# All of ff2 through the seven products, with weight sums added by DMA

## The chip, the cores and the metric

The kernel runs on 1 core of a Trainium2 chip. The metric is the device time of one execution in microseconds; below it is that of the profiled execution and the median of three others. TensorE (PE) multiplies, VectorE (DVE) and ScalarE (ACT) work element by element, GpSimd (POOL) does a few small operations, and transfers are issued by SyncE (SP) and carried by 16 DMA engines.

## The reference, cut to what matters

One layer on 512 tokens of 1024 channels: a gated pair of attention branches, a squared-ReLU MLP with 4096 hidden channels, a gated per-layer embedding, and norms between them. All is float32.

```python
u = rms_norm(h, g_mix[i])
z = u @ w_in[i]                      # q, k, v of both branches, forget logits, 2 x 1024 gate logits
# y_a, y_b: the two attention branches, each projected to 1024
gates = jax.nn.sigmoid(gate_logits).reshape(B, S, N_BRANCH, D_MODEL)
mixed = gates[:, :, 0] * y_a + gates[:, :, 1] * y_b
h = h + mixed @ w_mix_out[i]
u = rms_norm(h, g_mlp[i])
h = h + jnp.square(jax.nn.relu(u @ w_ff1[i])) @ w_ff2[i]      # 1024 -> 4096 -> 1024
ple_gate = jax.nn.sigmoid(rms_norm(h, g_ple[i]) @ w_ple_gate[i])
h = h + ple_gate * (p[i] @ w_ple_proj[i])
return rms_norm(h, g_final)
```

## The kernel before, in words

Every operand of a matmul is split into a high and a low half (`hi_lo`, lines 72 to 75: ScalarE casts the high half, VectorE subtracts for the low one), and a product is three passes: high times high, high times low, low times high (`mm3`). A weight is loaded by SP into a raw tile (`emit_dma`, lines 221 to 237), and `emit_split` (278 to 303) makes its two halves in `w_hi` and `w_lo`, tiles with four buffers each. A *unit* is one such weight; `order` is their sequence, `advance(i)` splits up to unit i, and `look["n"]` counts the units split. Raw tiles are 1 MB and stand in two rings of two (`w_raw`, `w2_raw`); loads are asked for three units ahead.

Some large products go through a scheme with seven products in place of eight: input and weight are cut into 2 x 2 blocks, seven sums of blocks are multiplied (numbers 1 to 7, `pn`), and three accumulators x, y and z in PSUM collect them (`win_mm`, `win_out`). The sums of weight blocks are made by VectorE in `sum_source` (251 to 276), one 1024-column operation each: two for product 6, one each for 7 and 4. The gates' upper half (`P2_STEPS`) and all of ff1 work so.

The MLP is done in four quarters `fq` of 1024 hidden channels, each two groups of 512 (`2 * fq` and `2 * fq + 1`). ff1 of both groups takes 14 products of 24 matmuls with 256 columns. `ff1_act` applies ReLU and square on ScalarE, `ff1_lo` makes the low halves and, for the even group, the sums that ff2's seven products need. ff2 of the even group takes seven products (`s2_mm`, 12 matmuls of 512 columns each); ff2 of the odd group is done plainly (`ff2_mm`): 4 row blocks by 2 halves, 12 matmuls each, in the same or a fourth accumulator. `h_add` adds the accumulators to `h_sb` on VectorE. In the last quarter the plain part goes by row blocks, so that the squares for the last norm (`part_ssq`) and the transposes `t3` follow block by block; then come the gate products `psgt` with the weights `wpg`.

The order on PE and POOL is written out by hand; `FIRST_STEPS` and `NEXT_STEPS` (lines 45 to 50) give that of the products, and in the loop of lines 1283 to 1322 step n splits the units up to step n + 2 and forms sums up to n + 3. ACT, DVE and SP are ordered by a planner, except in the stretches under `manual_schedule` (lines 1264 to 1322 up to n = 2, among others). Ahead of the loop stands the entry: the last row block of the mix product, the transposes of the normed rows (`t2_pe`), the sums of their blocks (`t2_sums`, `t2_sums2`, `t2_rest`, partly on POOL) and the embedding product (`pp_half`), whose results `ppo` are spilled and reloaded as `pp`.

Of the kernel before, what the change touches and what calls it, by code (L numbers as in the profile page):

```python
# [14 lines left out]
P = 128  # L15
# [29 lines left out]
FIRST_STEPS = ((1, 1), (0, 1), (0, 2), (1, 2), (0, 6), (0, 5), (0, 7), (1, 6), (0, 4), (0, 3),  # L45
               (1, 7), (1, 5), (1, 4), (2, 1), (1, 3), (2, 6), (2, 2), (2, 5), (2, 7), (2, 3),
               (2, 4))
NEXT_STEPS = ((0, 1), (0, 2), (0, 6), (1, 1), (1, 2), (0, 7), (0, 5), (0, 4), (0, 3), (1, 6),
              (2, 1), (1, 7), (1, 5), (2, 2), (1, 4), (1, 3), (2, 6), (2, 5), (2, 7), (2, 3),
              (2, 4))  # L50
# [4 lines left out]
def layer_kernel(ctx: ExitStack, tc: tile.TileContext, x, p, g_mix, w_in, b_forget, swa_sinks,  # L55
# [52 lines left out]
    def ff_steps(fq):  # L108


        a, b = 2 * fq, 2 * fq + 1
        first = [("s2", fq, pn) if i == 2 else ("f1", (a, b)[i], pn)
                 for i, pn in (NEXT_STEPS if fq else FIRST_STEPS)]
        last = []
        if fq < 3:
            last += [("f2", fq, ((half, j),), range(NT)) for half in range(2) for j in range(2)]
        else:
            last += [("f2", fq, ((0, 0), (0, 1), (1, 0), (1, 1)), (tb,)) for tb in range(NT)]
        return first + last

    steps = [st_ for fq in range(4) for st_ in ff_steps(fq)]
# [22 lines left out]
    def blocks(w, r0, c0, name):  # L144

        return [add_raw([(slice(0, 4), w[r:r + 512, c0:c0 + 512]
                          .rearrange("(k q) c -> q k c", q=P))], [P, 4, 512], f"{name}_{r}")
                for r in (r0, r0 + 512)]
# [23 lines left out]
    for fq in range(4):  # L172
        gw = {}
        for g in (2 * fq, 2 * fq + 1):
            gw[g] = blocks(w_ff1, 0, g * 512, f"wf1_{g}")
        c2 = [add_raw([(slice(0, 4), w_ff2[fq * 1024:fq * 1024 + 512, ch * 512:ch * 512 + 512]
                        .rearrange("(k q) c -> q k c", q=P))], [P, 4, 512], f"wf2_{fq}_{ch}")
              for ch in range(2)]
        f2 = [rows(w_ff2, fq * 1024 + 512, ch * 512, f"wf2b_{fq}_{ch}") for ch in range(2)]
        for st_ in ff_steps(fq):  # L180
            if st_[0] == "f1":
                add(st_, (gw[st_[1]], st_[2], [P, 4, 2, P]))
            elif st_[0] == "s2":
                add(st_, (c2, st_[2], [P, 2, 512]))
            else:
                for half, j in st_[2]:
                    if ("f2", fq, half, j) not in unit_of:
                        add(("f2", fq, half, j), f2[half][j])
# [5 lines left out]
    look = {"t2": None, "split": 2, "dma": 4, "wp2": None, "n": 0, "d": 0}  # L194

    def raws_of(i):
        r, pn = order[i][1][:2]
        if not isinstance(r, list):
            return [r]
        if order[i][0][0] in ("f1", "g"):  # L200
            return {1: r[:1], 2: r[1:], 3: r[1:], 4: r[1:]}.get(pn, r)
        return {1: r[:1], 2: r[:1], 3: r[1:], 4: r[:1], 5: r[:1], 7: r[1:]}.get(pn, r)
# [12 lines left out]
    in_wp2, same = [], {True: [], False: []}  # L215
    for n, r in enumerate(used):
        in_wp2.append(n >= first_raw[first_block] and (n - first_raw[first_block]) % 4 > 1)
        same[in_wp2[n]].append(n)
    before = {n: s_[z - 2] for s_ in same.values() for z, n in enumerate(s_) if z >= 2}

    def emit_dma(i):

        upto = max(first_raw[r] for r in raws_of(i))
        while look["d"] <= upto:
            n = look["d"]
            if n in before and last_use[used[before[n]]] >= look["n"]:
                return
            r = raws[used[n]]
            if in_wp2[n]:
                if look["wp2"] is None:  # L230
                    return
                r["tile"] = look["wp2"].tile(r["shape"], F32, tag="w2_raw", bufs=2, name=r["name"])
            else:
                r["tile"] = wp.tile(r["shape"], F32, tag="w_raw", bufs=2, name=r["name"])
            for ks, src in r["fns"]:
                nc.sync.dma_start(r["tile"][:, ks, :], src)
            look["d"] += 1

    def quadrant(i, h, e):

        rs = order[i][1][0]
        if order[i][0][0] in ("f1", "g"):
            t = raws[rs[h]]["tile"].rearrange("q k (j e c) -> q k j e c", e=2, c=P)
            return t[:, :, :, e]
        return raws[rs[e]]["tile"][:, h:4:2, :]
# [3 lines left out]
    def sum_source(i):  # L251

        if i in sources or i >= len(order) or not isinstance(order[i][1][0], list):
            return
        emit_dma(i)
        rs, pn, _ = order[i][1]

        first = {6: 1, 4: 2}.get(pn)
        if (first and unit_of[order[i][0][:-1] + (first,)] >= look["n"]
                or pn in (4, 7) and unit_of[order[i][0][:-1] + (6,)] not in sources  # L260
                or any(raws[r]["tile"] is None for r in raws_of(i))):
            return
        if pn == 6:
            b11, b12, b22 = quadrant(i, 0, 0), quadrant(i, 0, 1), quadrant(i, 1, 1)
            t1 = sources[unit_of[order[i][0][:-1] + (5,)]] = look.pop("t1", b11)
            nc.vector.tensor_tensor(t1, b12, b11, ALU.subtract)
            sources[i] = raws[rs[0]]["t2"] = look["t2"](order[i][1][2], f"t2_{i}")
            nc.vector.tensor_tensor(sources[i], b22, t1, ALU.subtract)  # L268
        elif pn == 7:
            b12 = sources[i] = quadrant(i, 0, 1)  # L270
            nc.vector.tensor_tensor(b12, quadrant(i, 1, 1), b12, ALU.subtract)
        elif pn == 4:
            b21 = sources[i] = quadrant(i, 1, 0)
            nc.vector.tensor_tensor(b21, b21, raws[rs[0]]["t2"], ALU.subtract)  # L274
        else:
            sources[i] = quadrant(i, pn in (2, 3), pn == 3)

    def emit_split(i):
# [8 lines left out]
        src = sources[i] if isinstance(r, list) else raws[r]["tile"][sl]  # L287
# [17 lines left out]
    def advance(i):  # L305

        while look["n"] < min(len(order), i + 1):
            emit_split(look["n"])
            look["n"] += 1
            emit_dma(min(len(order) - 1, look["n"] + 3))  # L310
# [32 lines left out]
    def to_uT(xn, uh, ul, tb, trp, name):  # L343

        for half in range(2):
            tr = trp.tile([P, 4, P], F32, tag="tr", bufs=3, name=f"{name}_tr{half}")
# [469 lines left out]

    at2 = ctx.enter_context(tc.tile_pool(name="at2", bufs=1))
# [40 lines left out]
    def win_out(key, pn, new):  # L858
# [30 lines left out]
    look["t2"] = lambda shape, name: hp.tile(shape, F32, tag="gb", bufs=1, name=name)  # L889
# [10 lines left out]
    def gate_ops(z):  # L900
# [21 lines left out]
        nc.vector.tensor_tensor(a12, a12, a22, ALU.subtract)  # L922
# [4 lines left out]
    def gate_out(res, gi):  # L927
# [3 lines left out]
        for j in range(2):  # L931
            m = 4 + 2 * j + e
# [4 lines left out]
            nc.scalar.activation(sgw[gi, m][:, 256 * i:256 * i + 256], src[:, j], AF.Sigmoid)  # L937
# [50 lines left out]
    look["t2"] = lambda shape, name: wk3.tile(shape, F32, tag="t2", bufs=1, name=name)  # L988
# [12 lines left out]
    def h_add(tb, half, ps):  # L1001
        sl = h_sb[:, tb, half * 512:half * 512 + 512]
        nc.vector.tensor_tensor(sl, ps, sl, ALU.add)  # L1003
# [20 lines left out]
    def new_op(pn):  # L1024
        n = (5, 7, 3).index(pn)
        u_op[pn] = [spare(n + 4 * i, f"u2_{pn}{'hl'[i]}", (P, 4, 256)) for i in range(2)]
# [25 lines left out]
    def put(pn, tb, src):  # L1052
        sl = t2_cols(tb)
        hi_lo(u_op[pn][0][sl], u_op[pn][1][sl], src)
# [9 lines left out]
    def t2_sums(tb):  # L1064
# [4 lines left out]
        nc.vector.tensor_tensor(s1, trs[tb, 1], a21, ALU.add)  # L1069
# [3 lines left out]
    def t2_sums2(tb):  # L1073
        a21, s1, s2, s3, s4 = sums[tb]
        nc.vector.tensor_tensor(s2, s1, a_raw[0][t2_cols(tb)], ALU.subtract)
        put(6, tb, s2)
        nc.gpsimd.tensor_tensor(s4, a_raw[1][t2_cols(tb)], s2, ALU.subtract)
# [26 lines left out]
    def pp_half(half):  # L1104

        wh, wl = unit(("pp", half))
        for tb in range(NT):
# [8 lines left out]
            if half == 1:  # L1116
                nc.sync.dma_start(pp_dram[tb], pp_out[tb])

# [315 lines left out]
```

## Time and profile before

| | |
|---|---|
| median of 3 runs | 746.66 us (745.09 to 746.82) |
| profiled execution | 745.08 us, span 743.4 us |
| PE, DVE, ACT, POOL busy | 98%, 74%, 58%, 5% of the span |
| DMA | 87.36 MB in 54584 packets, mean 118 GB/s |

The span runs from the first to the last instruction of the profiled execution; some 1.7 us of its time lie around it. In the rows further down, "a <-b" names the tile written and the tiles read, L is the line of the kernel, and an idle time stands with what ended it. Times in timelines and chains are microseconds from the start of the span.

### The profile page before, as it was taken

Reading aid. Unit: us, or ns where it says so; the run is one execution under the profiler, and the core shown is the slowest. Engines: PE = TensorE matmul, PEld = TensorE weight load, DVE = VectorE, ACT = ScalarE, POOL = GpSimd, SP = SyncE. Lnnn points to the kernel's source line nnn. Section 1 sums busy time; section 2 is a strip of 40 time slices with the busy share of each in tenths; the row PEclk is TensorE's granted clock in tenths of the full one; section 3 lists DMA queues with packets and bytes.
Section 4 is the critical chain, followed back from the end, with each engine's and each line's share of the span. In section 5 each row is a group of like instructions: output and inputs, shape, how many; then the busy total and the mean of one; then the engine's idle time right before and its main releaser. Section 6 shows DMA issues by size and latency. Waiting matters only on the chain.

```text
span 743.4 us, 11230 instructions
## 1 busy us (share of the span) xinstructions
PE 729.8 (98%) x4282; PEld 643.2 (87%) x4282; DVE 549.4 (74%) x906; ACT 431.1 (58%) x814; POOL 38.1 (5%) x71
## 2 busy tenths in 40 slices
PE   8999999999999999999999999999999999999996
PEld 7988888888889998887989889988999889988885
DVE  5656978876799557355989678985889578973654
ACT  6547888789753543335767317752486227754542
POOL 1011301100000000002100000000000000001001
PEclk9999999999999999999999999999999999999998
DMA  8266546550540382430242703252033603472002
GB/s 268 77 169 145 148 106 160 143 156 0 181 160 1 140 324 71 147 114 1 113 142 86 226 2 114 66 177 99 13 123 122 197 1 114 142 233 108 1 1 114
DMA packets 54584, 87.36 MB, mean 118 GB/s; under 512 B 5121, under 2 KB 22017, under 8 KB 54530
## 3 DMA queue, kind: packets, MB, share of 16 engines
q1 hardware_dynamic: 54530, 86.64, 37.1%
q8 instruction: 34, 0.56, 0.3%
q14 instruction: 20, 0.16, 0.1%
HBM read 72.93 MB, written 4.19 MB: 104 GB/s over the span
## 4 chain that ended last, share of the span: by engine, by line
PE 92%; DVE 4%; ACT 1%; DMA 1%; issue 1%; POOL 0%; SPq 0%; POOLq 0%; DVEq 0%; ACTq 0%
PE pf L78 5%; PE pf L80 5%; PE pf L79 5%; PE h_sc L700 2%; PE h_pv L770 2%; PE h_tr L758 2%; PE psm L78 2%; PE psm L80 2%; PE psm L79 2%; PE psy L80 2%; PE psy L78 2%; PE psy L79 2%; PE psgt L80 2%; PE psgt L78 2%; PE psgt L79 2%; PE va L433 2%
## 5 line engine op out<-in xcount | busy, mean ns | idle before, releaser
L718 ACT ACTIVATE s<-s,h_nm 128x128 f32<-128x128 f32 (+1 forms) x64 | 32.6, 512 | 5.9 <-DVE h_nm L711 5.2
L329 POOL TENSOR_SCALAR n_ms<-acc 128x1 f32<-128x1 f32 x15 | 4.9, 325 | 584.1 <-ACT junk L1011 518.2
L75 DVE TENSOR_TENSOR h_ptl<-h_tr,h_pth 128x512 fp32r<-128x512 f32 (+2 forms) x40 | 22.9, 604 | 3.9 <-ACT h_pth L74 3.6
L1011 ACT ACTIVATE junk<-h_sb 128x512 f32<-128x512 f32 x16 | 10.1, 632 | 21.9 <-DVE h_sb L1003 21.9
L74 ACT CAST u_h<-n_tr 128x512 fp32r<-128x512 f32 x22 | 12.3, 584 | 14.7 <-PE n_tr L349 7.8
L74 ACT CAST h_pth<-h_tr 128x512 fp32r<-128x512 f32 (+2 forms) x40 | 19.5, 523 | 1.8 <-PE h_tr L758 1.4
L75 DVE TENSOR_TENSOR u_l<-n_tr,u_h 128x512 fp32r<-128x512 f32 x22 | 14.7, 686 | 7.2 <-ACT u_h L74 7.1
L758 PE MATMUL h_tr<-ident,s 128*128 128x128 f32 x136 | 19.6, 277 | 0.2 <-ACT s L738 0.2
L1003 DVE TENSOR_TENSOR h_sb<-psm,h_sb 128x512 f32<-128x512 f32 x8 | 5.5, 689 | 16.3 <-PE psm L80 16.3
L1340 DVE TENSOR_TENSOR sgp<-sgp,pp 128x512 f32<-128x512 f32 (+1 forms) x9 | 5.7, 632 | 15.8 <-ACT sgp L1339 15.8
L770 PE MATMUL h_pv<-h_pth,v 128*128 128x256 f32 (+1 forms) x64 | 17.3, 291 | 0.0
L770 PE MATMUL h_pv<-h_ptl,v 128*128 128x256 f32 (+1 forms) x64 | 16.9, 305 | 0.4 <-DVE h_ptl L75 0.3
L758 PEld LDWEIGHTS h_tr<-ident,s 128*128 128x128 f32 x136 | 15.1, 141 | 2.0 <-ACT s L738 0.6
L738 ACT ACTIVATE s<-s,h_rec 128x128 f32<-128x128 f32 (+2 forms) x32 | 14.2, 483 | 2.3 <-DVE h_rec L732 2.3
L780 DVE TENSOR_TENSOR h_ao<-h_pv,h_ao 64x512 f32<-64x512 f32 x16 | 10.9, 681 | 6.1 <-ACT h_ao L779 5.8
L268 DVE TENSOR_TENSOR t<-wf,wf 128x1024 f32<-128x1024 f32 x12 | 14.6, 1218 | 0.1
L274 DVE TENSOR_TENSOR wf<-wf,t 128x1024 f32<-128x1024 f32 x12 | 14.6, 1215 | 0.0
L706 DVE CUSTOM_DVE_ANT_0 s<-h_sc,causal 128x128 f32<-128x128 f32 (+3 forms) x32 | 13.8, 483 | 0.3 <-PE h_sc L700 0.3
L732 DVE RECIPROCAL h_rec<-h_den 128x4 f32<-128x4 f32 x16 | 3.0, 185 | 14.5 <-ACT s L718 14.3
L770 PEld LDWEIGHTS h_pv<-h_ptl,v 128*128 128x128 f32 x64 | 12.1, 188 | 1.7 <-DVE h_ptl L75 0.8
L1339 ACT ACTIVATE sgp<-psgt,rs 128x512 f32<-128x512 f32 x7 | 4.8, 688 | 14.7 <-PE psgt L80 14.7
L706 DVE CUSTOM_DVE_ANT_0 s<-h_sc,bswa 128x256 f32<-128x256 f32 (+1 forms) x32 | 10.6, 383 | 3.1 <-PE h_sc L700 3.1
(1756 smaller groups left out, 2944.3 us busy)
## 6 DMA issues: line engine op xcount, KB each, us to landing
wf<-in_w_ff_dram SPq DMA_DIRECT2D x24, 1024.0 KB, 5.2
wf2b<-in_w_ff_dram SPq DMA_DIRECT2D x8, 1024.0 KB, 4.9
wg<-in_w_in_dram SPq DMA_DIRECT2D x4, 1024.0 KB, 5.7
wgw<-in_w_in_dram SPq DMA_DIRECT2D x4, 1024.0 KB, 5.7
wmix<-in_w_mix_out_dram SPq DMA_DIRECT2D x4, 1024.0 KB, 5.3
wpg<-in_w_ple_gate_dram SPq DMA_DIRECT2D x4, 1024.0 KB, 7.3
wv<-in_w_in_dram SPq DMA_DIRECT2D x4, 520.0 KB, 6.1
x<-in_x_dram SPq DMA_DIRECT2D x8, 256.0 KB, 4.5
```

The lines of the kernel that those rows point to most:

```text
L74: nc.scalar.copy(hi, src)
L75: nc.vector.tensor_tensor(lo, src, hi.bitcast(F32), ALU.subtract)
L78: nc.tensor.matmul(ps, lh, rh, start=start, stop=False)
L79: nc.tensor.matmul(ps, lh, rl, start=False, stop=False)
L80: nc.tensor.matmul(ps, ll, rh, start=False, stop=stop)
L268: nc.vector.tensor_tensor(sources[i], b22, t1, ALU.subtract)
L433: nc.tensor.matmul(ps, u[:, kk_, ts_], w[:, kk_, c0:c1], start=kk_ == 0 and n == 0, stop=kk_ == KT - 1 and n == 2)
L700: nc.tensor.matmul(ps[:, off:off + n], qs[i][z][:, qb * P:(qb + 1) * P], kk[i][z][:, k0:k0 + n], start=z == 0, stop=z == 1)
L706: nc.vector.tensor_tensor_reduce(out=s[:, o:o + n], in0=ps[:, off:off + n], in1=c["bias"](qb), scale=1.0, scalar=NEG, op0=ALU.add, op1=ALU ...
L718: nc.scalar.activation(sl, sl, AF.Exp, bias=nm[:, qb:qb + 1], accum_out=den[:, qb:qb + 1])
L758: nc.tensor.transpose(tr[:, n, :], c["s"][:, o, :], ident)
L770: nc.tensor.matmul(pv[:, q0:q0 + nq, :], V2[kb][:, c["v"], :], t[:, o:o + nq, :], start=n == 0, stop=n == 2 * NT - 1, skip_group_check=True)
```

## The change

- `STEPS` replaces the two step lists: per quarter 28 products, a and b being ff1 of the even and odd group, A and B their ff2. Both groups' ff2 goes through the seven products; the odd group adds into the accumulators that the even group began (`s2_mm`), and `h_add` follows only the odd group (`s2_out`). `ff2_mm` and the fourth accumulator go.
- The scheme's signs are turned so that sums of weights are additions. `sum_source` makes each sum in the place of one of its blocks: by a DMA from POOL that adds (`accum_op`), except products 5 and 7 of ff2, which stay on VectorE. The gates' weight sums become such DMAs too. They are formed as soon as the unit is split whose place they take (in `advance`).
- The ff weights come in 512 KB blocks, into twelve places of that size (eight halves of the old raw tiles and `t2`, `c3`, `c7`, `gb`), each given to the next block by the time that it comes free. Loads are asked for eight units ahead in the MLP.
- The operands of ff2 get fixed places `d0` to `d7` and one of `xn`; their sums are formed by `ff2_op` some steps after product 4 of ff1, for both groups.
- In the entry the splits of the first four units and the sums are spread among the row blocks of `pp_half`. The transposes `t3` move: 0 ahead of the last product, 1 behind it, 2 and 3 behind the first two row groups of `psgt`.

```diff
+STEPS = "a1 b1 a2 a5 b5 b2 a6 b6 a7 a3 b7 b3 A1 a4 b4 B1 A2 A5 B5 B2 A6 B6 A3 A7 B7 B3 A4 B4"
...
+    steps = [("f1" if c in "ab" else "s2", 2 * fq + (c in "bB"), int(pn))
+             for fq in range(4) for c, pn in STEPS.split()]
...
+    for g in range(8):
+        ff_blocks["f1", g] = block(w_ff1, 0, g * 512, 4, 256, f"wf1_{g}")
+        ff_blocks["s2", g] = block(w_ff2, g * 512, 0, 2, 512, f"wf2_{g}")
...
+            pl = min(free_at, key=free_at.get)
+            before[r] = free_at[pl]
+            free_at[pl] = last_use[r]
+            place_of[r] = pl
+        elif r >= last_ff:
+            w2 = sum(x >= last_ff for x in used[:n]) < 2
+            z = sum(x >= last_ff for x in used[:n]) % 2
+            before[r] = max(free_at[w2, z, y] for y in range(2))
...
-        if pn == 6:
-            b11, b12, b22 = quadrant(i, 0, 0), quadrant(i, 0, 1), quadrant(i, 1, 1)
-            t1 = sources[unit_of[order[i][0][:-1] + (5,)]] = look.pop("t1", b11)
-            nc.vector.tensor_tensor(t1, b12, b11, ALU.subtract)
-            sources[i] = raws[rs[0]]["t2"] = look["t2"](order[i][1][2], f"t2_{i}")
-            nc.vector.tensor_tensor(sources[i], b22, t1, ALU.subtract)
...
+        if pn in (1, 2, 3):
+            q = quadrant(i, pn in (2, 3), pn == 3)
         else:
-            sources[i] = quadrant(i, pn in (2, 3), pn == 3)
+            q = quadrant(i, 0, pn == 7)
+            other = quadrant(i, *{5: (0, 1), 7: (1, 1), 6: (1, 1), 4: (1, 0)}[pn])
+            if key[0] == "s2" and pn in (5, 7):
+                nc.vector.tensor_tensor(q, q, other, ALU.add)
+            else:
+                nc.gpsimd.dma_start(q, other, accum_op=ALU.add)
...
             look["n"] += 1
-            emit_dma(min(len(order) - 1, look["n"] + 3))
+            emit_dma(min(len(order) - 1, look["n"] + look["ahead"]))
+            if isinstance(order[n][1][0], (list, dict)):
+
+                key = order[n][0]
+                for pn in {1: (5,), 5: (6, 7), 6: (4,)}.get(key[-1], ()):
+                    if key[0] != "s2" or pn in (6, 4):
+                        sum_source(unit_of[key[:-1] + (pn,)])
...
+    look["ahead"] = 8
...
+    def ff2_op(g, pn):
+
+        r11, r12, r21, r22 = (rs_[g, i, e] for i in range(2) for e in range(2))
+        if pn == 5:
+            nc.vector.tensor_tensor(r22, r22, r21, ALU.subtract)
+            dst = r22
+        if pn == 6:
+            nc.vector.tensor_tensor(r21, r11, r21, ALU.subtract)
+            nc.vector.scalar_tensor_tensor(r11, r22, -1.0, r11, ALU.mult, ALU.subtract)
+            dst = r11
+        if pn == 7:
+            dst = r21
+        if pn == 3:
+            nc.vector.scalar_tensor_tensor(r12, r12, -1.0, r11, ALU.mult, ALU.subtract)
+            dst = r12
+        hi_lo(*new_ff2_op(g, pn), dst)
...
-    def s2_mm(fq, pn):
+    def s2_mm(g, pn):
 
         bk, tg = S2_TAGS[pn]
-        wh, wl = unit(("s2", fq, pn))
-        oh, ol = ops[2 * fq, pn]
+        tg = "" if g % 2 else tg
+        wh, wl = unit(("s2", g, pn))
+        oh, ol = ops[g, pn]
...
     look["split"] = 0
+    advance(f1_0)
     t2_sums(2)
     h2(3, 1, ps)
     t2_sums2(2)
     scale2(3)
-    pp_half(0)
-    advance(f1_0)
+    pp_half(0, {1: lambda: advance(f1_0 + 1)})
     t2_pe(3)
     t2_sums(3)
-    advance(f1_0 + 1)
-    pp_half(1)
-    t2_sums2(3)
-    advance(f1_0 + 2)
+    pp_half(1, {0: lambda: t2_sums2(3), 1: lambda: advance(f1_0 + 2), 2: lambda: t2_rest(5),
+                3: lambda: advance(f1_0 + 3)})
...
+                if done[2] == 4:
+                    for w, pn in ((1, 5), (1, 6), (5, 3), (6, 7)):
+                        later.setdefault(n + w, []).append((done[1], pn))
...
+        if n == len(steps) - 2:
+            t3(0)
         done = st_
         if n == 2:
             man.close()
-    ff2_out(3, 0, 3)
-    ff2_out(3, 1, 3)
+    s2_out(3, 4)
+    t3(1)
```

## Rows read from the trace of the kernel before

**Rows 1.** The page, part 1: busy time, share, instructions.

```profile
PE 729.8 (98%) x4282; PEld 643.2 (87%) x4282; DVE 549.4 (74%) x906; ACT 431.1 (58%) x814; POOL 38.1 (5%) x71
```

**Rows 2.** Busy time by stretch: the entry, and one middle quarter.

```profile
core 0: us, PE busy (x) PEld busy (x) DVE busy (x) ACT busy (x) POOL busy (x), PEclk, DMA share, GB/s
...
345.00:383.70 38.70, 35.65 (x242) 32.78 (x241) 35.45 (x38) 27.44 (x43) 6.13 (x5) 0.96 0.23 83
...
442.80:524.80 82.00, 82.00 (x519) 73.67 (x518) 66.11 (x74) 44.39 (x58) 0.00 (x0) 1.00 0.32 103
```

**Rows 3.** Waits of TensorE, 300 to 400 us: total, times, longest.

```profile
PE ('f1', 1)x L854 <- ACT ppo L1115: 1.0, 1, 1.0
PE ('f1', 1)x L854 <- ACT u60h L301: 0.9, 1, 0.9
PE ('f1', 1)x L854 <- DVE u60l L302: 0.8, 1, 0.8
PE n_tr L1047 <- DVE n_xn L339: 0.3, 1, 0.3
```

**Rows 4.** The chain of waits in the entry: start, length, what.

```profile
371.69 0.60 DVE o L1192
...
373.50 1.14 DVE wf L274
...
378.08 1.23 DVE u60l L302
...
379.36 4.39 PE ('f1', 1)x L854 x22
```

**Rows 5.** The chain of waits in a quarter: ff1, ff2's seven, plain.

```profile
442.81 2.86 PE ('f1', 2)x L854 x24
...
471.44 2.80 PE s_1x L1219 x12
...
502.38 2.80 PE s_1y L1244 x12
```

**Rows 6.** The page, part 6: loads, KB each, us to landing.

```profile
wf<-in_w_ff_dram SPq DMA_DIRECT2D x24, 1024.0 KB, 5.2
...
wpg<-in_w_ple_gate_dram SPq DMA_DIRECT2D x4, 1024.0 KB, 7.3
...
h_sb<-in_x_dram SPq DMA_DIRECT2D x1, 2048.0 KB, 10.1
...
pp<-pp_spill SPq DMA_DIRECT2D x4, 512.0 KB, 6.0
...
wpp<-in_w_ple_proj_dram SPq DMA_DIRECT2D x2, 512.0 KB, 3.3
```

**Rows 7.** Waits of all engines, the whole span.

```profile
ACT u105h L301 <- PE f_1w L1244: 4.6, 1, 4.6
```

**Rows 8.** Groups of instructions in the quarter: a weight's cast and low half.

```profile
L301 ACT CAST u81h<-wf 128x1024 fp32r<-128x1024 f32 x1 | 1.0, 1048 | 4.6 <-PE f_0w L1244 4.6
...
L302 DVE TENSOR_TENSOR u81l<-wf,u81h 128x1024 fp32r<-128x1024 f32 x1 | 1.2, 1226 | 0.4 <-ACT u81h L301 0.4
```

**Rows 9.** DMA queues in the quarter: packets, MB, share of 16 engines.

```profile
q1 hardware_dynamic: 4224, 8.39, 31.7%
```

**Rows 10.** The chain of waits at the first gate product.

```profile
691.38 0.23 PE psgt L78
```

**Rows 11.** Timelines of ACT and DVE, 684 to 700 us: gate weights.

```profile
686.39 1.34 ACT L292 ACTIVATE u153h<-wpg,g_ple_t 128x512 fp32r<-128x512 f32 x2 [0.21 <-ACT u_h L74]
...
694.19 0.74 DVE L293 SCALAR_TENSOR_TENSOR u156l<-wpg,g_ple_t,u156h 128x512 fp32r<-128x512 f32 x1
```

**Rows 12.** Timelines of POOL and DVE in the entry: overlapping operations.

```profile
358.57 1.62 POOL L1077 TENSOR_TENSOR u_s<-u_a,u_s 128x512 f32<-128x512 f32 x1 [4.34 <-DVE u_s L1075]
...
358.95 1.80 DVE L75 TENSOR_TENSOR u_5l<-u_s,u_5h 128x512 fp32r<-128x512 f32 x1
```

More of the change, by code (lines that the diff above doesn't have):

```diff
@@ L106, in rows, with block @@
                 for j in range(nk // 2)]
[L108 to L121, printed above, removed]
+    def block(w, r0, c0, nk, nc_, name):
+        return {(h, e): add_raw([(slice(0, nk), w[r0 + h * nk * P:r0 + (h + 1) * nk * P,
+                                                  c0 + e * nc_:c0 + (e + 1) * nc_]
+                                  .rearrange("(k q) c -> q k c", q=P))], [P, nk, nc_],
+                                f"{name}_{h}{e}") for h in range(2) for e in range(2)}
+    steps = [("f1" if c in "ab" else "s2", 2 * fq + (c in "bB"), int(pn))
+             for fq in range(4) for c, pn in STEPS.split()]
     def add(key, spec):
@@ L171, in layer_kernel @@
         add(("pp", half), rows(w_ple_proj, 0, half * 512, f"wpp{half}", 2)[0])
[L172 to L188, printed above, removed]
+    first_ff = len(raws)
+    ff_blocks = {}
+    for g in range(8):
+        ff_blocks["f1", g] = block(w_ff1, 0, g * 512, 4, 256, f"wf1_{g}")
+        ff_blocks["s2", g] = block(w_ff2, g * 512, 0, 2, 512, f"wf2_{g}")
+    last_ff = len(raws)
+    for st_ in steps:
+        add(st_, (ff_blocks[st_[:2]], st_[2], [P, 4, 2, P] if st_[0] == "f1" else [P, 2, 512]))
     for half in range(2):
@@ L192, in layer_kernel @@
                 add(("pg", half, 2 * r4 + j), u)
-    look = {"t2": None, "split": 2, "dma": 4, "wp2": None, "n": 0, "d": 0}
+    look = {"split": 2, "dma": 4, "ahead": 3, "wp2": None, "n": 0, "d": 0}
     def raws_of(i):
         r, pn = order[i][1][:2]
[L198 to L202, printed above, removed]
+        if isinstance(r, dict):
+            return [r[z] for z in {1: ((0, 0),), 2: ((1, 0),), 3: ((1, 1),),
+                                   5: ((0, 0), (0, 1)), 6: ((0, 0), (1, 1)),
+                                   7: ((0, 1), (1, 1)), 4: ((0, 0), (1, 0))}[pn]]
+        if isinstance(r, list):
+            return {1: r[:1], 2: r[1:], 3: r[1:]}.get(pn, r)
+        return [r]
     used, last_use = [], {}
@@ L224, in emit_dma @@
         while look["d"] <= upto:
-            n = look["d"]
-            if n in before and last_use[used[before[n]]] >= look["n"]:
+            r_ = used[look["d"]]
+            r = raws[r_]
+            if r_ in before and before[r_] >= look["n"]:
                 return
-            r = raws[used[n]]
-            if in_wp2[n]:
+            if first_ff <= r_ < last_ff:
+                if "place" not in look:
+                    return
+                r["tile"] = ff_place(place_of[r_], r["shape"])
+            elif place_of[r_]:
                 if look["wp2"] is None:
@@ L254, in sum_source @@
             return
         emit_dma(i)
[L256 to L260, printed above, removed]
+        key, (rs, pn, _), _ = order[i]
+        first = {5: 1, 6: 5, 4: 6}.get(pn)
+        if (first and unit_of[key[:-1] + (first,)] >= look["n"]
+                or pn == 7 and unit_of[key[:-1] + (5,)] not in sources
                 or any(raws[r]["tile"] is None for r in raws_of(i))):
@@ L999, in row_group, with h_add @@
         return ps
-    def h_add(tb, half, ps):
+    def h_add(tb, half, ps, sign=1.0):
         sl = h_sb[:, tb, half * 512:half * 512 + 512]
-        nc.vector.tensor_tensor(sl, ps, sl, ALU.add)
+        if sign > 0:
+            nc.vector.tensor_tensor(sl, ps, sl, ALU.add)
+        else:
+            nc.vector.scalar_tensor_tensor(sl, ps, sign, sl, ALU.mult, ALU.add)
     def accs_of(nm):
@@ L1024, in new_op @@
     def new_op(pn):
[L1025 to L1026 removed]
+        u_op[pn] = [spare(c, f"u2_{pn}{'hl'[i]}", (P, 4, 256))
+                    for i, c in enumerate({5: (0, 1), 7: (2, 6), 3: (4, 5)}[pn])]
     for n, places in enumerate(((0, 1), (2, 6))):
@@ L1102, in p_transposed, with pp_half @@
                   ptl[:, k, :].rearrange("q (t c) -> q t c", c=P), tr)
-    def pp_half(half):
+    def pp_half(half, between):
         wh, wl = unit(("pp", half))
```

251 lines of the change are left out of this document (117 added, 134 removed), and 6 rows, old and new, of the table P2_STEPS.

## The prediction

> **What bounds the kernel now.** I read the busy shares first: TensorE is busy 98% of the span, VectorE 74% [rows 1]. An average says little of a stage, so the table by stretches came next. In one middle quarter of the MLP (442.8 to 524.8 us) TensorE is busy 82.00 us of 82.00, at granted clock 1.00, while VectorE has 66.11 us in 74 instructions [rows 2]. The waits of TensorE between 300 and 400 us are four and add up to 3.0 us [rows 3]; from 400 us to the end the same view has none. So from about 384 us the MLP's length is the number of its products times their length. The one place where something else sets the pace is the entry: in 345 to 383.7 us TensorE has 35.65 of 38.70 us at clock 0.96, VectorE 35.45 [rows 2]. There the chain of waits runs through VectorE, among it weight sums of 1.14 us each, up to `u60l`, for which TensorE waits; the product behind it takes 4.39 us for 22 of its 24 matmuls, where 2.86 is usual [rows 4, 5]: part of it at 1.2 GHz instead of 2.4, after the engine had waited.
>
> **The change, part by part.** The sum is made against the profiled execution, 745.08 us; the median of the three runs, 746.66, lies 1.6 us above it.
>
> *Products.* A quarter is now 14 ff1 products, 7 of ff2 and 8 plain pieces of 12 matmuls: 29 steps of 2.80 to 2.88 us [rows 5]. `STEPS` has 28: the 8 plain pieces become 7 products of 12 matmuls with the same 512 columns. That is 12 matmuls or 2.80 us less in each of four quarters: -11.2 us, all on the engine that sets the end.
>
> *VectorE in a quarter.* Before: 25 low halves and 12 weight sums of 1024 columns, and 37 operations of 512 columns (6 of `win_out`, 4 operand sums, 11 low halves of operands, 16 additions to `h_sb`); 37 and 37 make the 74. After: 28 low halves and 4 sums (ff2's products 5 and 7), and 42 small ones (6, 8, 14 and 14). Five long ones at 1.14 us go, five short ones at 0.60 [rows 4] come: 66.1 - 2.7 = 63.4 us, in a quarter of 79.2. The same share (80%), so no bound. ScalarE gets three 1024-column casts and three short ones more, about 5 us on 44.4 [rows 2]: no bound.
>
> *Sums by DMA.* A quarter has 12 (ff1's 5, 6, 7 and 4 for two groups, ff2's 6 and 4), each adding 512 KB inside SBUF. No adding transfer is in the trace. From below, the nearest is a plain 512 KB load, 3.3 us to landing. From above: it reads two operands and writes one, as if 1.5 MB, half-way between 5.2 us for 1 MB and 10.1 for 2 MB, 7.7 us, behind one load of 5.2: 12.9 us [rows 6]. I take 6, what the 512 KB reload of `pp` shows [rows 6].
>
> What delay may a sum have? The four buffers of `w_hi` let a weight be split three steps ahead of its product (a cast waits for TensorE to give one back [rows 7]), and a split takes 1.05 + 1.23, some 2.3 us [rows 8]. Product 5 stands three steps behind product 1, product 6 three behind 5, and each needs one sum made in the place just split. From the start of product 1's step, 6 is split at -8.5 + 3 x 2.3 + 2L = 2L - 1.6, and is wanted at 6 x 2.83 = 17.0: L may be 9.3 us without a stall. For ff2's 5 to 6, one sum, it may be 12.4. At 6 us the sums cost nothing; the cover is the three steps of lead, and if it is gone each us of L over 9.3 costs 2 us per quarter, 8 in all.
>
> *The transfers' room.* Loads take 31.7% of the sixteen DMA engines over the 82 us, 26 us for 8.4 MB [rows 9], so 3.1 us per MB. 6.3 MB of sums add 20 us at one pass, 39 at two: 58 to 83% of 79.2 us. It fits, but a sum can find loads in its way. The Trainium skill (DMA: Bandwidth & Descriptors, "Issuing engines are not separate DMA queues") says that transfers issued from different engines end up on the same 16 DMA engines and interleave, so the POOL queue gives the sums no lane of their own. The same page (section "Anatomy of one DMA") fits 2.0 us plus bytes over 436 GB/s for transfers issued from POOL, about 3.2 us for 512 KB by my estimate; no run here shows it. The loads themselves are asked for eight units ahead instead of three, into twelve places of 512 KB: about 22 us of lead against 3.3 to 6 us. Nothing.
>
> *POOL.* Each sum queues there behind the wait for its split. Only in the entry does anything else stand behind it: the two subtractions of `t2_sums` and `t2_sums2` and the norm's power, on which `t2_pe(3)` already waits 0.3 us [rows 3].
>
> *Entry.* Eight sums of 1.14 us leave a VectorE that is full there, and ff1 starts with weights split earlier (`advance(f1_0)` ahead of `t2_sums(2)`). At best the 3.0 us of waits and the 1.5 us of slow clock go: -4.6. At worst the sums sit on POOL in front of the norm: +3, one plain transfer's time. I take -3.0, since two of the three large waits hang on the VectorE chain [rows 3, 4] and the third on a copy that is still there. What is late next is that copy of `ppo`.
>
> *Tail.* The transposes of `u3` are the same number, two earlier. But `wpg` (the first two loads) now takes places whose last reader is B4's split, the last of all, some 8.5 us before the end of B4; before, they were loaded long ahead. Landing takes 5.2 to 7.3 us [rows 6], so the first split starts 3.2 to 1.1 us ahead of that end, 4.1 to 2.0 ahead of the first `psgt`, with eight transposes between (0.87 us). Before, it starts at 686.39, 5.0 us ahead of `psgt` at 691.38 [rows 10, 11]; the fourth ends at 694.93 [rows 11] and is wanted after 18 matmuls of 0.23 us [rows 10], at 695.6, with 0.7 to spare. Now it is 0.2 to 2.3 us late. Bounds 0 to +4; the upper end adds a second load that shares the engines with the first. I take +1.5, a little over the middle of 0.2 to 2.3.
>
> *The rest.* Signs move into operations that exist (`scale=-1.0`, scalar_tensor_tensor for tensor_tensor): nothing, VectorE's slack hides them. The gates' new order has the same 14 products in a gapless stretch, its first weights are split two 5.6 us steps ahead, and eight sums leave VectorE: nothing; bounds as for L.
>
> Sum: 745.1 - 11.2 - 3.0 + 1.5 = 732.4. Half of the 1.6 us by which the median lies above goes on top: **733 us**.
>
> **The rivals.** (a) *The adding transfers come too late*: slower. Place: the casts of products 5 and 6 in ff1, behind which ScalarE and VectorE queue in order and for which TensorE then waits. It loses all once L reaches 9.3 + 12.7/8 = 10.9 us; at 12, 8 x 2.7 = 21.6 us are lost: 754; at the upper bound 12.9, with ff2's 4 x 0.5, 763. For: up to 83% DMA share, bursts of loads; against: single loads of this size land in 3.3 to 6 us.
> (b) *VectorE becomes the bound because POOL holds it up.* Where POOL's subtraction runs 1.62 us, a VectorE operation that takes 0.60 elsewhere lasts 1.80 [rows 12]. Twelve sums at 1.1 us more are 13 us: 76.8 of 79.2, still hidden. If each holds VectorE for a whole 1.62 us, 63.4 + 19.4 = 82.8: +3.6 per quarter, 732.4 + 14.4 = 747. By a page of the Trainium skill (SBUF — State Buffer, "Who interferes with whom") an operation with two SBUF inputs is held up only by a POOL instruction that reads SBUF; rows 12 agree, since that subtraction reads. The section "SBUF: two separate sides" adds that writing descriptors stalls beside two-port copies on VectorE, and no run here shows that; this kernel's large copies are on ScalarE [rows 8].
> (c) *The entry or the tail eats part*: the entry at +3, the tail at +4, 740.
> (d) *Nothing is saved*, because something just under TensorE takes over at once: 745. Against it: VectorE at 80%.
>
> **How the numbers follow.** Forecast 0.62 (728 to 737), (c) 0.10, (b) 0.10, (a) 0.16, (d) 0.02. Under 728 only if the entry gives all and the tail nothing: 745.1 - 11.2 - 4.6 = 729.3, less the spread of runs. The range 727 to 747 leaves out (a) and a little of (b). About 0.3%, 2.2 us, is what a measurement of this kernel can tell from no change: faster (under 744.4) takes the forecast, (c) and half of (b), 0.77; within, (d) and part of (b), 0.06; slower 0.17.
>
> **What would show it.** Right: a quarter between two like ff1 steps of 79.2 us with no wait of TensorE; VectorE near 63 us in it; adding transfers landing in under 9 us; the 4.39 us product gone. Wrong: waits of TensorE on casts whose own wait is an adding transfer (a); VectorE's 1024-column operations well over 1.2 us and VectorE full (b); a wait at the first `psgt` over 4 us (c).

## The result, and the profile after

The changed kernel takes 737.76 us, median of 4 runs (736.25 to 738.64); the kernel before, on the same chip, 746.74 us. The ratio is 0.9883, 95% interval [0.9861, 0.9904]: 9.0 us or 1.2% faster. The forecast was 733, range 727 to 747. The spans of the two traced executions are 743.4 and 734.2 us, 9.2 apart.

The page of the profile after, part 1 (busy time, share, instructions), answers [rows 1]:

```profile
PE 721.4 (98%) x4234; PEld 635.9 (87%) x4234; DVE 530.7 (72%) x898; ACT 449.5 (61%) x838; POOL 86.2 (12%) x127
```

The stretches that answer [rows 2], the entry and two middle quarters:

```profile
core 0: us, PE busy (x) PEld busy (x) DVE busy (x) ACT busy (x) POOL busy (x), PEclk, DMA share, GB/s
345.00:384.20 39.20, 37.09 (x261) 34.16 (x258) 26.88 (x32) 27.25 (x44) 13.49 (x14) 1.00 0.84 205
440.71:519.89 79.18, 79.18 (x506) 71.55 (x506) 63.70 (x75) 48.91 (x64) 10.37 (x12) 1.00 0.74 188
519.89:599.07 79.18, 79.18 (x506) 71.55 (x506) 63.70 (x75) 48.97 (x64) 10.38 (x12) 1.00 0.73 187
```

A quarter is 79.18 us, TensorE busy in all of it, VectorE 63.70; forecast were 79.2 and 63.4. In the entry VectorE fell from 35.45 us to 26.88, and the DMA share rose from 0.23 to 0.84. The transfers of one quarter, answering [rows 9] (queue, packets, MB, share of 16 engines; below, KB each and median us to landing for seven of the twelve sums, then the landing of all twelve):

```profile
q0 software_dynamic: 1758, 6.42, 42.8%
q1 hardware_dynamic: 6400, 8.39, 31.4%
...
wq<-wq POOLq DMA_DIRECT2D x7, 512.0 KB, 5.2
...
DMA to landing us min/median/max: 4.4/5.5/9.3
```

q0 carries the adding transfers: 6.42 MB take 42.8% of 79.18 us, 33.9 us or 5.3 per MB, against 3.0 for the loads on q1. The twelve land in 4.4 to 9.3 us, median 5.5, where 6 was taken. TensorE's waits from 300 us to the end, answering [rows 3]:

```profile
PE ('f1', 0)x L884 <- ACT u_('f1', 0)_4210 L895: 1.8, 1, 1.8
PE n_tr L1085 <- DVE n_xn L368: 0.3, 1, 0.3
```

Three of the four old waits are gone and a new one has come. The chain ahead of it, answering [rows 4]:

```profile
366.84 0.96 ACT u57h L323
367.80 0.02 issue
367.82 1.24 DVE u57l L324
369.06 0.29 issue
369.35 7.31 DMA wq<-wq
...
376.68 1.06 ACT u60h L323
...
378.90 1.22 DVE u61l L324
...
382.61 1.04 ACT u63h L323
383.65 0.49 ACT u_('f1', 0)_4210 L895
...
384.18 3.09 PE ('f1', 0)x L884 x24
```

The sum for product 6 is added in the place that `u57` was split from; it takes 7.31 us, and the cast `u60h` waits for it. ScalarE's operations follow each other in order, so the copy (`u_`, L895) for which TensorE waits comes late with that cast. The copy saves accumulator x of the first group as it stands after product 6, and product 7 may add to x only after that.

**Where the 9 us come from.** Four marks of both traces, in us: the last `h_pv` (start of the program), the first product of the second quarter, the last GpSimd operation (`n_l_rs`), the end.

| stretch | before | after | difference | predicted |
|---|---|---|---|---|
| to the last `h_pv` | 194.84 | 198.09 | +3.25 | 0 |
| from there to the second quarter | 247.97 | 242.62 | -5.35 | -2.8 - 3.0 |
| three quarters and the tail | 295.85 | 287.49 | -8.36 | -8.4 + 1.5 |
| from the last GpSimd operation | 4.74 | 6.00 | +1.26 | 0 |

In this pair the two middle stretches, -13.7 together, exceed the -12.7 worked out, and what is missing was lost at the start, where the program is the same, and in the last 6 us. Part of the -13.7 is luck, as the second traces show. The experiments ask what is chance, what the adding transfers are worth, and how near to too late they are.

### The profile page after: what moved, and what is told of

It is laid out like the page before. It is cut to its first block, busy times and chain, and to the rows that moved or that the text cites. A ratio compares the mean times of both kernels' runs of the same rounds, so it can differ in the third digit from the quotient of the medians.

```text
span 734.2 us, 11456 instructions
## 1 busy us (share of the span) xinstructions
PE 721.4 (98%) x4234; PEld 635.9 (87%) x4234; DVE 530.7 (72%) x898; ACT 449.5 (61%) x838; POOL 86.2 (12%) x127
## 3 DMA queue, kind: packets, MB, share of 16 engines
q0 software_dynamic: 8064, 29.36, 21.0%
## 4 chain that ended last, share of the span: by engine, by line
PE 94%; DVE 2%; ACT 2%; DMA 1%; issue 1%; POOL 0%; POOLq 0%; DVEq 0%; ACTq 0%
PE pf L73 5%; PE pf L75 5%; PE pf L74 5%; PE s_6x L1269 3%; PE s_4x L1269 3%; PE s_2x L1269 3%; PE s_0x L1269 3%; PE h_sc L729 2%; PE h_pv L799 2%; PE h_tr L787 2%; PE psy L73 2%; PE psy L75 2%; PE psy L74 2%; PE psm L74 2%; PE psm L75 2%; PE psm L73 2%
## 5 line engine op out<-in xcount | busy, mean ns | idle before, releaser
L297 POOL DMA_DIRECT2D wq<-wq x26 | 23.5, 941 | 177.5 <-DVE u154l L324 27.1
L69 ACT CAST u_h<-n_tr 128x512 fp32r<-128x512 f32 x22 | 12.2, 584 | 15.5 <-PE n_tr L378 7.6
L297 POOL DMA_DIRECT2D wgw<-wgw x8 | 7.1, 970 | 101.7 <-DVE u25l L324 77.7
L767 ACT ACTIVATE s<-s,h_rec 128x128 f32<-128x128 f32 (+2 forms) x32 | 14.2, 483 | 2.3 <-DVE h_rec L761 2.3
L735 DVE CUSTOM_DVE_ANT_0 s<-h_sc,causal 128x128 f32<-128x128 f32 (+3 forms) x32 | 13.8, 483 | 0.3 <-PE h_sc L729 0.3
L1357 ACT ACTIVATE sgp<-psgt,rs 128x512 f32<-128x512 f32 x7 | 4.8, 685 | 14.2 <-PE psgt L75 14.2
L799 PEld LDWEIGHTS h_pv<-h_pth,v 128*128 128x128 f32 x64 | 12.1, 189 | 0.9
```

The source lines that it names most:

```text
L69: nc.scalar.copy(hi, src)
L297: nc.gpsimd.dma_start(q, other, accum_op=ALU.add)
L767: nc.scalar.activation(sl, sl, AF.Copy, scale=rec[:, qb:qb + 1])
L799: nc.tensor.matmul(pv[:, q0:q0 + nq, :], V2[kb][:, c["v"], :], t[:, o:o + nq, :], start=n == 0, stop=n == 2 * NT - 1, skip_group_check=True)
```

## The experiments

**The changed kernel again, and the kernel before again.** Nothing edited.

> The changed kernel once more, nothing edited. Its first traced execution was 3.3 us late at the last h_pv (198.09 against 194.84 in the kernel before), although the instructions up to there are the same: its TensorE stayed at the low clock to about 13.5 us instead of 6. Theory (chance of one execution): this time the start-up may fall either way; over five rounds the median lies between 734 and 738, and a traced execution with an early rise of the clock has its last h_pv near 194.8 and a span near 731. Rival (the changed program starts late every time): last h_pv again near 198.1 and the span near 734.2.

> The kernel before once more, nothing edited. Traces so far: it and the kernel with two sums on VectorE had TensorE at the high clock from about 6 us (last h_pv at 194.84 and 195.18), the changed kernel twice and two of its variants from about 13 us (197.7 to 198.1). Theory (chance, the same for every kernel here): the last h_pv falls at either 194.8 to 195.2 or 197.7 to 198.1, whichever this time. Rival (each program has its own): 194.8 again; one trace more can only speak against the rival, not prove it. Second reading: the time from the last output's issue to the end of the span is 2.9 us again, against 4.0 to 4.2 in all kernels with adding transfers.

The first gave 736.27 us (731.76 to 737.82, 6 runs; ratio 0.9855 [0.9824, 0.9886]) with a traced span of 735.5 us; the second 743.44 us in its single run, span 741.7. The two groups of products of the start, in the traces of before, of after, and of the kernel with two sums on VectorE (line, engine, operation, tiles, count, busy us, mean ns, idle before):

```profile
L461 PE MATMUL g_ps<-g_row,ones_row 1*128 1x512 f32 x4 | 2.0, 614 | 0.0
L465 PE MATMUL warm<-ident 128*128 128x128 f32 x14 | 1.8, 277 | 0.0
```

```profile
L490 PE MATMUL g_ps<-g_row,ones_row 1*128 1x512 f32 x4 | 3.8, 1096 | 0.0
...
L494 PE MATMUL warm<-ident 128*128 128x128 f32 x14 | 3.2, 425 | 0.0
```

```profile
L490 PE MATMUL g_ps<-g_row,ones_row 1*128 1x512 f32 x4 | 2.1, 652 | 0.0
L494 PE MATMUL warm<-ident 128*128 128x128 f32 x14 | 1.8, 277 | 0.0
```

The same 18 matmuls take 3.8 us in one execution and 7.0 in another. The column of the granted clock prints 1.00 for both stretches, but it has nothing to go by there: in the trace itself the record of the clock begins at 4.7 us before and at 13.8 us after, with 1.00. Ahead of that the matmuls are 1.5 to 1.8 times as long, so the late start fits a TensorE that stays at 1.2 GHz for some 8 us more. Among eleven traces five start early (last `h_pv` at 194.65 to 195.18, first entry of the clock at 4.7 to 5.8) and six late (197.71 to 198.17, first entry at 12.7 to 13.9). Programs with adding transfers stand on both sides, and the one without them that is tested below starts late, so the late start isn't theirs. That the kernel before starts late too is not shown, as both its traces are early; its other spans of 745.0 to 746.6 us suggest it.

A second chance effect stands in the entry. The product behind the wait is 3.09 us in the first trace of the changed kernel and 4.63 in the second; before, 4.39 in the first [rows 4] and 2.90 in the second. The chains of the two second traces, before and after:

```profile
379.18 2.90 PE ('f1', 1)x L854 x22
```

```profile
383.91 4.63 PE ('f1', 0)x L884 x24
```

The granted clock of 379 to 389 us is 0.83 in the two long cases and 1.00 in the two short ones: after waits just ahead of it of 1.7 to 1.9 us in sum, part of the product runs at 1.2 GHz in some executions and not in others, worth 1.5 us. From the last `h_pv` to the end, the change is worth 11.0 us with this product fast in both (547.1 to 536.1 us) and 10.8 with it slow in both (548.5 to 537.8). The 9.2 us between the first two traces mix a late start with a product that was slow before and fast after.

**All weight sums on VectorE.** The condition in `sum_source` always takes the VectorE branch:

```diff
-            if key[0] == "s2" and pn in (5, 7):
+            if True:
```

> All weight sums are formed on VectorE, none by an adding transfer; the 28 products per quarter stay. VectorE in a quarter: 63.7 us plus 12 sums of 1.22 us = 78.3 of 79.2 us. Theory A (the gain of the quarters comes from the eight plain pieces, the adding transfers only make room on VectorE, and that room is needed where VectorE would be 99% busy): quarters of 79.2 to 81 us, the entry loses its 3 us again; 3 to 10 us over the changed kernel, so 741 to 748. Theory B (the adding transfers are what saves): all 9 us or more are lost, 747 or more. Theory C (their place doesn't matter): the changed kernel's time within 1.5 us.

It took 745.65 us (743.57 to 747.81, 12 runs; ratio to before 0.9991 [0.9973, 1.001]): nothing is left of the gain, though 48 matmuls are saved. Two stretches of a quarter's length (from 17 us into the second), two pieces of the first of them, and the longest wait of TensorE in the third and second quarter (the others have the same):

```profile
460.11:542.19 82.08, 79.97 (x506) 71.33 (x505) 76.51 (x86) 49.23 (x64) 0.00 (x0) 1.00 0.33 103
542.19:624.28 82.09, 79.97 (x506) 71.33 (x505) 76.50 (x86) 49.22 (x64) 0.00 (x0) 1.00 0.30 97
...
460.00:470.00 10.00, 10.00 (x87) 10.00 (x86) 5.89 (x7) 7.11 (x10) 0.00 (x0) 1.00 0.72 224
475.00:510.00 35.00, 33.01 (x174) 27.55 (x174) 35.00 (x44) 22.30 (x30) 0.00 (x0) 1.00 0.21 65
```

```profile
PE s_4z L1269 <- DVE u131l L324: 1.8, 1, 1.8
PE s_2z L1269 <- DVE u103l L324: 1.8, 1, 1.8
```

A quarter is 82.08 us, as long as before with 29 products. Expectation A's quarter (79.2 to 81) was too short, its total (741 to 748) right. VectorE's 76.5 of 82.1 us is an average: from 475 to 510 us it is busy without a break, and at 508 us TensorE waits 1.8 us for `u103l`, while from 460 to 470 us it has room that doesn't help there. So the products earn nothing without the transfers. The transfers without the products were not run; as the quarter before has no wait of TensorE, only the entry could gain by them.

**Where the entry's wait comes from.** First, the sums of product 6 of the first two groups go to VectorE:

```diff
-            if key[0] == "s2" and pn in (5, 7):
+            if key[0] == "s2" and pn in (5, 7) or key[:2] in (("f1", 0), ("f1", 1)) and pn == 6:
```

> Only the sums of product 6 of ff1's first two groups (two of them) are formed on VectorE instead of by adding transfers. In the changed kernel's trace the last wait of TensorE in the entry, 1.8 us on the last window of group 0, hangs on an adding transfer of 7.3 us from u57's split to u60's cast. Theory (in the entry the transfers come too late by a little): the wait goes or shrinks to under 0.5 us, and the product of 3.09 us behind it is 2.83: 1.5 to 2.0 us faster than the changed kernel. Rival (VectorE is what the entry waits for): two sums of 1.2 us on it move the wait later, 0 to 1 us slower.

It took 730.99 us (730.32 to 733.74, 6 runs; ratio to before 0.9803 [0.9774, 0.9833]). Its only wait of TensorE after 300 us:

```profile
PE n_tr L1085 <- DVE n_xn L368: 0.3, 1, 0.3
```

The wait is gone. From the last `h_pv` to the end it is 533.86 us, against 536.12 and 537.76 in the two traces of the changed kernel: 2.3 and 3.9 less, the wait without and with its slow clock. The median is 5.3 below the 736.27 of the changed kernel; early and late starts are mixed in both.

Second, the same splits earlier, with the transfers kept:

```diff
-    pp_half(1, {0: lambda: t2_sums2(3), 1: lambda: advance(f1_0 + 2), 2: lambda: t2_rest(5),
-                3: lambda: advance(f1_0 + 3)})
+    pp_half(1, {0: lambda: t2_sums2(3), 1: lambda: advance(f1_0 + 3), 2: lambda: t2_rest(5)})
...
-        if n in (2, 4):
-            t2_rest({2: 7, 4: 3}[n])
+        if n == 4:
+            t2_rest(3)
         if n > 0:
-            advance(last_unit(n + 2))
+            advance(last_unit(n + (3 if n == 1 else 2)))
+        if n == 2:
+            t2_rest(7)
```

> The weights of product 1 and 5 of ff1's first two groups are split one place earlier in the order of ScalarE and VectorE (u56 ahead of the operand's product-5 halves, u57 and u58 ahead of its product-7 halves); the adding transfers stay. Theory (the transfer's late start, not its length, makes the 1.8 us wait): the transfers start 2 to 4 us earlier, the wait on the first group's last window goes, 1.5 to 2.0 us faster. Rival (the operand halves that now come later are the next wait): a wait on an operand of product 7 or 3 of 1 to 3 us takes its place, and the time is the same or up to 2 us slower.

It took 733.25 us (732.58 to 737.96, 6 runs), 3.0 under the changed kernel's 736.27; but both spread over more than 5 us and overlap, and an early start alone is worth 3.3. Its trace, of a run of 737.87 us, decides more: the wait is still there, and the transfer starts 2.83 us earlier and ends as late.

```profile
PE ('f1', 0)x L884 <- ACT u_('f1', 0)_4210 L895: 2.1, 1, 2.1
```

```profile
366.52 10.44 DMA wq<-wq
```

Both expectations failed in that trace; the runs near 733 us were not traced. An earlier start doesn't help: the 16 DMA engines are full. The queues of 355 to 385 us in the changed kernel:

```profile
q0 software_dynamic: 1008, 3.67, 63.5%
q1 hardware_dynamic: 1721, 3.93, 36.6%
```

That is 100%, with four spills of `ppo`, weight loads and seven sums at once; the transfer asked for earlier only took longer. What helped was to form the two sums that are waited for on VectorE. The engines stay nearly full in that kernel (47.7% and 46.2% from 352 to 382 us), so moving these two sums is shown to help; that fewer bytes from elsewhere would do as well is not shown.

**Is TensorE alone the bound in a quarter?** The matmuls of one product, ff2's product 7 of the odd group, are left out in each quarter:

```diff
-            for j in range(2):
+            for j in range(0 if g % 2 and pn == 7 else 2):
```

> The changed kernel without the matmuls of ff2's product 7 for the odd row group of each quarter: 12 of 336 matmul positions per quarter are left out, everything else (its weight's load, sum, split, and the additions to h_sb) stays. Theory (TensorE alone sets the quarter): each quarter from the second on is 2.80 us shorter, 79.18 to 76.38 us, no wait of TensorE; about 11 us off the changed kernel's time. Rival (VectorE or the adding transfers are just under TensorE and take over): under 1.5 us per quarter is saved, and waits of TensorE on a low half or a cast appear.

It took 726.08 us (2 runs). The second and third quarters:

```profile
434.63:512.79 78.16, 76.63 (x494) 69.35 (x492) 63.32 (x75) 48.55 (x64) 10.37 (x12) 1.00 0.77 194
512.79:589.17 76.38, 76.38 (x494) 69.29 (x493) 63.34 (x75) 48.64 (x64) 10.38 (x12) 1.00 0.77 194
```

The third lost the whole 2.80 us. The second lost 1.0 and waited 1.5 us in ff1 on such a copy of x, as the entry does; ahead of it the cast of product 6 waits 2.3 us for an adding transfer. There the sums are the next bound.

**How late may a sum be?** Each adding transfer of ff1's products 5 and 6 in quarters 2 to 4 is held back by tiny additions on GpSimd that read the low half just made: 7 in one kernel, 15 in the other.

```diff
+                if key[0] == "f1" and key[1] > 1 and pn in (5, 6):
+                    lo = order[unit_of[key[:-1] + (first,)]][2][1]
+                    pad = sm.tile([P, 1], F32, tag="pad", bufs=1, name=f"pad_{i}")
+                    nc.gpsimd.tensor_scalar(pad, lo[:, 0, 0, 0:1].bitcast(F32), 1.0, None, ALU.add)
+                    for _ in range(6):     # 14 in the other
+                        nc.gpsimd.tensor_scalar(pad, pad, 1.0, None, ALU.add)
                 nc.gpsimd.dma_start(q, other, accum_op=ALU.add)
```

> Each adding transfer of ff1's products 5 and 6 in quarters 2 to 4 is held back on GpSimd by seven one-element additions of about 0.39 us, +2.8 us, once its operand is there: landing plus delay some 8.1 us instead of 5.3. Theory (the prediction's budget of 9.3 us from split to sum holds): quarters stay at 79.2 us, no wait of TensorE there; the changed kernel's time within 1 us. Rival (the budget is smaller, as casts stand in one order on ScalarE): each us costs up to 2 us per quarter, 3 to 5 us per quarter.

> The same with fifteen additions, +5.8 us: landing plus delay some 11.1 us, 1.8 us over the budget of 9.3. Theory (two sums in a row on one place, product 1 to 5 to 6, and TensorE waits for what they are late): 2 x 1.8 = 3.6 us longer quarters 2 to 4, 82.8 us, with a wait of TensorE at product 6; 8 to 14 us over the changed kernel, as the clock may fall after a wait. Rival (the splits run further ahead than three steps, so more room than 9.3 us): under 1 us per quarter.

They took 753.25 and 765.22 us (2 runs each; ratios to before 1.0107 [1.006, 1.0155] and 1.0268 [1.022, 1.0315]), far over what was expected. Quarters 2 and 3 with 7 additions, then with 15:

```profile
443.50:525.98 82.48, 79.93 (x505) 72.02 (x504) 63.53 (x75) 48.73 (x64) 19.28 (x41) 1.00 0.72 179
525.98:611.55 85.57, 81.91 (x505) 73.59 (x504) 63.52 (x75) 48.72 (x64) 19.48 (x41) 0.98 0.70 173
```

```profile
439.08:527.43 88.35, 82.83 (x506) 73.78 (x505) 63.44 (x75) 48.68 (x64) 25.41 (x73) 0.98 0.68 167
527.43:616.69 89.26, 82.68 (x505) 73.75 (x504) 63.38 (x75) 48.68 (x64) 26.40 (x73) 0.98 0.67 165
```

The delays were larger than planned, because the additions of two groups queue behind each other on GpSimd. What counts is the whole time from a low half's end to the cast that takes the sum. For group 5's products 1, 5 and 6 (units 110, 113, 116) it is read from VectorE's and ScalarE's timelines; of the changed kernel:

```profile
515.41 1.23 DVE L324 TENSOR_TENSOR u110l<-wq,u110h 128x1024 fp32r<-128x1024 f32 x1 [0.33 <-ACT u110h L323]
...
523.75 1.23 DVE L324 TENSOR_TENSOR u113l<-wq,u113h 128x1024 fp32r<-128x1024 f32 x1 [1.51 <-ACT u113h L323]
```

```profile
522.66 1.05 ACT L323 CAST u113h<-wq 128x1024 fp32r<-128x1024 f32 x1 [1.69 <-PE ('f1', 4)x L884]
...
532.59 1.05 ACT L323 CAST u116h<-wq 128x1024 fp32r<-128x1024 f32 x1 [1.27 <-DMA wq<-wq]
```

516.64 to 522.66 and 524.98 to 532.59: 6.0 and 7.6, together 13.6 us, and the product starts at 539.76, 6.1 us after `u116h` is made. With 7 additions, read in the same way, it is 9.6 and 12.2, together 21.8, against the budget of twice 9.3 = 18.6: 3.2 over, and TensorE waits 2.6 there (`u116h` 1.8, `u116l` 0.8). With 15 it is 14.2 and 11.5, together 25.7: 7.1 over, and it waits 1.4 at `u113` and 4.3 at `u116`. So the budget holds within about 1.5 us, and the expectations of the time failed by the size of the delay and by what follows a wait: in the quarter of 85.57 us, 3.7 us are waits and 2.7 us are products that run longer (PE busy 81.91 instead of 79.18, clock 0.98).

**A version without the two-step chain.** As the kernel with two sums moved, and ff1's sums 5 and 6 of quarters 2 to 4 on VectorE too:

```diff
-            if key[0] == "s2" and pn in (5, 7):
+            if (key[0] == "s2" and pn in (5, 7) or key[:2] in (("f1", 0), ("f1", 1)) and pn == 6
+                    or key[0] == "f1" and key[1] > 1 and pn in (5, 6)):
```

> As the kernel with the first two groups' product-6 sums on VectorE, and in quarters 2 to 4 ff1's sums 5 and 6 (four per quarter) on VectorE too; ff1's 7 and 4, ff2's 6 and 4 and the gates' sums stay adding transfers. VectorE 63.7 + 4 x 1.22 = 68.6 us of a 79.2 us quarter. Theory (TensorE sets the pace as long as VectorE has slack where it is needed): quarters 79.2 us, the time of the kernel with two sums moved, 731, within 1 us. Rival (VectorE's slack lies only in ff2's stretch, and in ff1's a sum on it is late at once): 0.5 to 2.9 us per quarter longer, 732 to 740.

It took 730.98 us (728.96 to 732.82, 6 runs; ratio to before 0.9803 [0.9773, 0.9834]), as the theory had it. A quarter:

```profile
438.18:517.36 79.18, 79.18 (x506) 71.55 (x505) 68.34 (x79) 48.91 (x64) 6.87 (x9) 1.00 0.60 160
```

VectorE has 68.34 us, as worked out (68.6), the DMA share falls from 0.74 to 0.60, and TensorE has no wait in it. This kernel and the one with two sums moved are some 15.7 us faster than the kernel before and the best complete ones here. The runs of each fall into two clusters 3.3 us apart, the early and the late start: spans 728.5 to 729.3 and 731.9 there, 727.3 to 727.8 and 730.8 to 731.1 here. Cluster against cluster this one is about 1.1 us ahead, most of it in the last stretch (below).

## Why the prediction was right, and where it was off

**Right: products and VectorE.** Quarters of 79.18 us without a wait, 2.82 shorter; VectorE at 63.70. Leaving out one more product took 2.80 off the third quarter: TensorE sets the pace.

**Right: L and its budget.** A median of 5.5 us was measured where 6 was taken, on 74% of the DMA engines' time where 58 to 83% was worked out. The kernels with delayed sums show that rival (a) decides where the forecast put it, two sums in a row over some 18.6 us, and what it costs there: 15 us with 7 additions, 27 with 15. But L is not one number: in the quarter's ff1 stretch, where several sums are issued close together, product 6 had to wait up to 7.3 us for its own and product 7, which comes later, up to 9.3, a little over the 9 named as a sign of being right; in the entry sums took up to 9.5.

**Off: the entry.** -3.0 was forecast; -2.55 came in the first pair of traces (-5.35 less the 2.80 of the products) and +0.56 in the second (-2.24 + 2.80). Both are coloured by the clock: the first pair had the product slow before and fast after, the second the other way round. Like against like, the stretch from the last `h_pv` to the second quarter goes from 246.51 to 242.62 us with the product fast, from 247.97 to 244.27 with it slow. So the entry gave 1.1 or 0.9 us, a third of the forecast, and -2.55 was luck. The waits agree: 3.0 us before, 2.1 after. The step that failed is what is late next: the prediction named the copy of `ppo`, but it was a sum of product 6. The budget of 9.3 us was worked out for a quarter, and in the entry the DMA engines are full, so rival (a) came true at this one place. The two sums on VectorE got back 2.3 to 3.9 us.

**Wrong: the tail.** +1.5 was forecast for late gate weights, 0.1 came (287.49 against 295.85 - 8.46). The step that failed is that the first two loads of `wpg` take places whose last reader is the last split of ff2. SyncE's waits for the places from 661 to 670 us, its loads, the casts, and the chain at the first `psgt`, answering [rows 10, 11]:

```profile
SPq L264 <- DVE u164l L324: 2.3, 1, 2.3
...
SPq L264 <- DVE u162l L324: 0.9, 1, 0.9
SPq L264 <- DVE u163l L324: 0.7, 1, 0.7
```

```profile
665.61 4.23 SPq L264 DMA_DIRECT2D wpg<-in_w_ple_gate_dram  x3
```

```profile
667.13 1.05 ACT L323 CAST u164h<-wq 128x1024 fp32r<-128x1024 f32 x1 [1.75 <-PE s_6x L1269]
673.68 0.72 ACT L314 ACTIVATE u165h<-wpg,g_ple_t 128x512 fp32r<-128x512 f32 x1 [0.95 <-DMA wpg<-in_w_ple_gate_dram]
```

```profile
679.13 0.87 PE n_tr L378 x8
680.01 0.23 PE psgt L73
```

`u164` is the last split, and only one of the four loads waits for it, the last to be issued. The load that the cast of `u165h` waits for, by its semaphore in the trace, goes out at 665.61, when `u162l` is done: 13.5 us ahead of the end of ff2 at 679.13, where 8.5 was taken. It lands after 8.0 us, in a stretch of many loads, where 5.2 to 7.3 was taken, and still the first cast is 6.3 us ahead of `psgt`; before it was 5.0.

**Off: two terms that had no place in the sum.** The start, +3.25 in the traced pair, is chance of the execution. The end, +1.26, is not, by the traces so far: from the issue of the last output to the end it is 4.17 us, in six of seven programs that add by DMA 4.01 to 4.17; in both traces of before and with all sums on VectorE it is 2.87 to 3.04. The exception is the kernel without the chain, 3.14 us, which adds fewer times (22.02 MB on q0 instead of 29.36). Why is open.

**Rivals.** (b) is refuted: VectorE's 1024-column operations take 1.22 to 1.23 us in a quarter with twelve sums issued by GpSimd, as before [rows 8]. (c) came true in part, as the entry kept a third of its gain, (d) not at all; but with all sums on VectorE (d) is what happens, in the place that it named.

The forecast of 733 was 4.8 under the median, within its range. In the profiled execution, 736.25 us against the sum's 732.4, the misses are 3.25 at the start, 1.3 at the end, 0.45 in the entry and 0.4 outside the span, less 1.4 in the tail. That the entry misses so little here is luck; like against like it misses 2 us, which the tail happens to cover in part. By their spans (eight of ten at 734.2 us or more) most runs of the changed kernel start late; two of them were traced.

A few sums in the prediction are off without changing anything: 3.0 + 1.5 is 4.5 and not 4.6 for the entry's best, 39 us of sums fill 82% and not 83%, and twelve sums at 1.1 us more give 76.6 and not 76.8.

## What to carry to other kernels

Saved TensorE time counts only if each engine that feeds it has room in the same stretch: here VectorE, 93% busy over a quarter but 100% over the 35 us around the waits, took back all that the products gave, and 12 sums moved to the DMA engines gave it back. A transfer's cost is read from the DMA share of its own stretch: in quarters at 0.74 the sums cost nothing, at 1.00 asking earlier bought nothing and making two sums elsewhere did. Before a gain of 1% is explained, the same kernel should be traced twice and like compared with like: two chance effects of 3.3 and 1.5 us stand in these traces under an unchanged program.

## What the runs showed of the hardware

An adding transfer inside SBUF costs its bytes nearly twice: 5.3 us of the 16 engines per MB, against 3.0 for a load. Sums of 512 KB issued close together take longer to land: the four that the changed kernel issues from 522.53 to 525.81 us land in 4.5, 6.7, 7.0 and 9.1 us, where the shortest in a quarter takes 4.4. Where the engines are full they take up to 12.4 us (the kernel with the early splits, 351 to 384 us). Issuing one takes GpSimd 0.86 us, 1.21 for some, with no mark on VectorE's durations.

In eleven traces of the same opening the record of TensorE's clock at 2.4 GHz begins either at 4.7 to 5.8 us or at 12.7 to 13.9 us, and the late beginning goes with a loss of 3.3 us. In eight of these traces TensorE waits 1.7 to 2.1 us in the entry; in four of them the clock falls to 1.2 GHz right after, worth 1.5 us, in the other four it stays at 2.4.
